# One split of 2,048 columns instead of two of 1,024 for each half chunk of expert weights

## The chip, the cores and the metric

The kernel runs on one core of one Trainium2 chip. A core has TensorE (PE in the profile; PEld is its weight load, which overlaps the matmuls), VectorE (DVE), ScalarE (ACT), GpSimd (POOL) and SyncE (SP, which issues the transfers), each with its own instruction stream; 16 DMA engines move data. The metric is the time of one execution in microseconds (us). Before the change it is 2620.03 us, the median of three runs between 2617.26 and 2626.58. One more execution was profiled; it took 2622.45 us, of which 2620.7 us is the span from the first to the last instruction and 1.75 us lies around it.

## The reference, cut to what matters

The program is a backbone of two layers over 256 context and 256 latent tokens of width 1024, in float32. Each layer mixes tokens and then channels; in the second layer the channel mixer is a set of eight experts, of which each token uses two. Only the experts matter here:

```python
D_MODEL, SEQ, N_EXPERTS, TOP_K, D_EXPERT = 1024, 256, 8, 2, 3584

def swiglu(h, w1, w3, w2):
    return (jax.nn.silu(h @ w1) * (h @ w3)) @ w2

def moe_swiglu(h, router, w1, w3, w2):
    logits = (h @ router).astype(jnp.float32)
    top_v, top_i = lax.top_k(logits, TOP_K)
    top_w = jax.nn.softmax(top_v, axis=-1)
    comb = jnp.einsum("blk,blke->ble", top_w,
                      jax.nn.one_hot(top_i, N_EXPERTS, dtype=jnp.float32)).astype(h.dtype)
    out = comb[..., 0:1] * swiglu(h, w1[0], w3[0], w2[0])
    for e in range(1, N_EXPERTS):
        out = out + comb[..., e:e + 1] * swiglu(h, w1[e], w3[e], w2[e])
    return out
```

Here h holds the 256 latent tokens. w1 and w3 are 1024 x 3584 for each expert and w2 is 3584 x 1024, so the eight experts have 352 MB of float32 weights, each read once.

## The kernel before, in words

The experts' stage is the last one of the program. It begins at about 1566 us of the span and ends with a short normalisation. The experts are taken in order of their number of tokens. Position 0, the largest, has up to 192 tokens in two groups, one of 128 and one of 64; positions 1 to 3 have up to 128, positions 4 to 7 up to 64. `gather` collects an expert's tokens with matmuls against a 0/1 matrix and casts them to two parts, a high and a low one. A group of 128 tokens is called heavy here; its high and low part are two tiles. A group of 64 is called light: both parts lie side by side in one tile of 128 columns.

Each expert is worked in seven chunks of 512 hidden columns. A chunk needs w1, w3 and w2 of these columns, two megabytes each, and each of them comes as two half chunks of 128 x 2048 float32 (one megabyte). That makes 6 loads for a chunk, 42 for an expert and 336 in all. `mload` is called once for each: SP issues the transfer into a landing tile `mland` (5 buffers), and `split` (lines 113 and 114) makes two tiles of the float32 data that a fast matmul can take: ScalarE casts it to the high part `mwh`, then VectorE subtracts this from the source and writes the rest, `mwl`. Before the change this is done in two steps of 1,024 columns, with 8 buffers for each of the two names. A buffer of `mwh` or `mwl` comes free when the last matmul that reads it is done, and only then can the cast of a later half begin.

TensorE multiplies the tokens by both parts. A heavy group takes three matmuls of 512 columns for each slice of weights (`mm3`, lines 121 to 123: high x high, high x low, low x high), a light group two (line 1152). One half of 1,024 columns carries 6 heavy or 4 light matmuls. `up1` multiplies by w1 and ScalarE copies the result out (line 1172 heavy, line 1174 light). `up3` multiplies by w3; for a light group ScalarE copies it out (line 1191), TensorE folds the two parts with 16 short matmuls (line 1195), ScalarE applies the silu (line 1198), VectorE multiplies (line 1199) and the product is split (`gh`). `down` multiplies by w2 into `y`. `back` spreads the sums back to the tokens.

The order of the work is not written out by hand. `steps` walks positions 1, 4, 2, 5, 3, 6, 7 so that `down` of a chunk stands behind `up1` of the next, and `experts` puts the fourteen steps of position 0 (`steps0`, whose `down` holds both half chunks of w2 for both groups) between those of the light positions. Then the tile framework's scheduler, which runs a cost model of its own, sets the order of the instructions in each engine's stream, and each engine works its stream strictly in that order.

Of the kernel before, what the change touches and what calls it, by code (L numbers as in the profile page):

```python
# [11 lines left out]
FR = mybir.dt.float32r  # L12
# [68 lines left out]
class Net:  # L81
# [1051 lines left out]
    def mload(self, src):  # L1133

        nc, p = self.nc, self.ep
        w = p.tile([128, 2048], FT, name="mland", tag="mland", bufs=5)
        nc.sync.dma_start(w, src)
        r = []
        for q in range(2):
            h = p.tile([128, 1024], FR, name="mwh", tag="mwh", bufs=8)  # L1140
            lo = p.tile([128, 1024], FR, name="mwl", tag="mwl", bufs=8)
            self.split(h, lo, w[:, q * 1024:(q + 1) * 1024])
            r.append((h, lo))
        return r

    def mmx(self, o, x, i, w, start, stop):

# [426 lines left out]
```

## Time and profile before

| what | value |
|---|---|
| median of 3 runs | 2620.03 us |
| profiled execution | 2622.45 us |
| its span | 2620.7 us |
| experts' stage | about 1566 to 2608 us of the span |
| PE busy, whole span | 2370.6 us, 90% |
| DVE busy, whole span | 2159.9 us, 82% |
| ACT busy, whole span | 1374.9 us, 52% |
| transfers of expert weights | 336 of 1 MB, median 6.5 us from issue to landing |

The busy share of an engine is an average over the whole program; what a change in the experts' stage can do is read from stretches inside it, and from what ended each idle time there. A matmul's row gives an end that is modelled, and neighbouring matmuls overlap, so the distance between two starts is what TensorE really spends on one. The same holds, to a smaller degree, for instructions of VectorE and ScalarE that stand back to back.

### The profile page before, as it was taken

The numbers are of one execution on the slowest core, as the hardware profiler recorded it, in microseconds if no ns is written. First come the engines' busy times: TensorE is split into PE (matmuls) and PEld (weight loads), VectorE is DVE, ScalarE is ACT, GpSimd is POOL, SyncE is SP. The second block draws the span as 40 slices with busy tenths as digits, with TensorE's granted clock in tenths as the row PEclk, the third lists the DMA queues.
The fourth block names the chain that finished last, engine by engine and source line by source line (L and its number), as shares of the span: only waits on it lengthen the run. The fifth ranks groups of instructions, "written<-read, shape, count | busy, mean of one in ns | idle before, by whom it ended". The sixth has DMA issues, their size and how long they took to land. (4 is left out here: it accounts for less than half of the span.)

```text
span 2620.7 us, 35146 instructions
## 1 busy us (share of the span) xinstructions
PE 2370.6 (90%) x12456; PEld 1947.5 (74%) x12456; DVE 2159.9 (82%) x3182; ACT 1374.9 (52%) x1965; POOL 190.1 (7%) x210
## 2 busy tenths in 40 slices
PE   7968978999999999987878969999999999999986
PEld 2746765788777877767768968888888788888775
DVE  8877699974767988976889678888988889898897
ACT  3334332323353233324544527777877677787864
POOL 1540000000100023221000010000000000000000
PEclk8978988999999999998989978999999999999988
DMA  6555423652234556674544529998899889999984
GB/s 239 165 181 113 145 89 125 205 161 82 96 91 159 179 163 193 204 244 115 175 137 130 178 86 348 356 358 335 344 353 350 326 332 344 354 361 365 359 325 203
DMA packets 157017, 594.11 MB, mean 227 GB/s; under 512 B 46423, under 2 KB 55321, under 8 KB 113825
## 3 DMA queue, kind: packets, MB, share of 16 engines
q1 hardware_dynamic: 156832, 591.79, 64.0%
q8 instruction: 99, 1.62, 0.2%
q14 instruction: 86, 0.70, 0.1%
HBM read 560.29 MB, written 31.42 MB: 226 GB/s over the span
## 5 line engine op out<-in xcount | busy, mean ns | idle before, releaser
L114 DVE TENSOR_TENSOR mwl<-mland,mwh 128x1024 fp32r<-128x1024 f32 x672 | 788.8, 1220 | 83.1 <-ACT mwh L113 71.6
L113 ACT CAST mwh<-mland 128x1024 fp32r<-128x1024 f32 x672 | 675.6, 1051 | 131.2 <-PE mp L123 42.0
L113 ACT CAST wh<-land 128x512 fp32r<-128x512 f32 x396 | 244.9, 621 | 525.7 <-PE p L122 238.2
L114 DVE TENSOR_TENSOR wl<-land,wh 128x512 fp32r<-128x512 f32 x396 | 294.5, 748 | 133.4 <-ACT wh L113 130.1
L121 PE MATMUL p<-hh,wh 128*128 128x256 f32 (+1 forms) x800 | 274.9, 345 | 7.4 <-DVE q L547 3.0
L123 PE MATMUL p<-hh,wl 128*128 128x256 f32 (+1 forms) x800 | 273.7, 344 | 2.8 <-DVE wl L114 2.7
L122 PE MATMUL p<-hl,wh 128*128 128x256 f32 (+1 forms) x800 | 272.6, 342 | 0.1
L1152 PE MATMUL mp<-mwl,xg 128*128 128x512 f32 x560 | 224.3, 403 | 4.2 <-DVE mwl L114 4.2
L1152 PE MATMUL mp<-mwh,xg 128*128 128x512 f32 x560 | 222.6, 400 | 3.3 <-ACT mwh L113 2.6
L121 PE MATMUL mp<-mwh,xg 128*128 128x512 f32 x448 | 179.4, 401 | 2.6 <-ACT mwh L113 2.6
L122 PE MATMUL mp<-mwl,xg 128*128 128x512 f32 x448 | 178.3, 398 | 2.2 <-DVE mwl L114 2.2
L123 PE MATMUL mp<-mwh,xg 128*128 128x512 f32 x448 | 176.7, 394 | 0.0
L121 PEld LDWEIGHTS p<-hh,wh 128*128 128x128 f32 x800 | 155.2, 194 | 27.8 <-ACT wh L113 3.9
L785 DVE SCALAR_TENSOR_TENSOR ma<-mw,sv,ma 128x512 f32<-128x512 f32 x196 | 150.5, 792 | 28.4 <-DMA mw<-in_w_mod 28.1
L123 PEld LDWEIGHTS p<-hh,wl 128*128 128x128 f32 x800 | 154.3, 193 | 22.9 <-DVE wl L114 5.5
L122 PEld LDWEIGHTS p<-hl,wh 128*128 128x128 f32 x800 | 154.8, 194 | 15.7 <-DVE hl L749 0.3
L123 PE MATMUL fo<-hh,wl 128*128 128x512 f32 (+1 forms) x384 | 146.9, 384 | 6.6 <-DVE wl L114 6.6
L121 PE MATMUL fo<-hh,wh 128*128 128x512 f32 (+1 forms) x384 | 146.9, 383 | 1.4 <-ACT hh L745 0.9
L122 PE MATMUL fo<-hl,wh 128*128 128x512 f32 (+1 forms) x384 | 145.6, 380 | 0.0
L667 DVE SCALAR_TENSOR_TENSOR dc<-ub,cfp,dc 128x512 f32<-128x512 f32 (+1 forms) x240 | 138.2, 614 | 0.5
L1152 PEld LDWEIGHTS mp<-mwl,xg 128*128 128x128 f32 x560 | 107.3, 192 | 27.4 <-DVE mwl L114 6.6
L1152 PEld LDWEIGHTS mp<-mwh,xg 128*128 128x128 f32 x560 | 107.3, 192 | 24.7 <-ACT mwh L113 4.5
(462 smaller groups left out, 4717.4 us busy)
## 6 DMA issues: line engine op xcount, KB each, us to landing
mland<-in_moe_w SPq DMA_DIRECT2D x336, 1024.0 KB, 6.5
mw<-in_w_mod SPq DMA_DIRECT2D x96, 512.0 KB, 4.5
land<-in_w_in SPq DMA_DIRECT2D x96, 512.0 KB, 4.3
land<-in_ffn_w SPq DMA_DIRECT2D x66, 512.0 KB, 3.6
land<-in_w_bo SPq DMA_DIRECT2D x24, 512.0 KB, 3.4
s5wc<-sw SPq DMA_DIRECT2D x16, 512.0 KB, 3.9
s5we<-weT SPq DMA_DIRECT2D x16, 512.0 KB, 3.6
we<-s5we SPq DMA_DIRECT2D x16, 512.0 KB, 4.4
```

The source lines that it names most:

```text
L113: nc.scalar.copy(h, src)
L114: nc.vector.tensor_sub(lo, src, h.bitcast(FT))
L121: nc.tensor.matmul(o, a[0], b[0], start=start, stop=False)
L122: nc.tensor.matmul(o, a[0], b[1], start=False, stop=False)
L123: nc.tensor.matmul(o, a[1], b[0], start=False, stop=stop)
L667: nc.vector.scalar_tensor_tensor(d, ub[:, :R, i:i + 64], cfp[:, j, i:i + 1], d, op0=OP.mult, op1=OP.add)
L785: nc.vector.scalar_tensor_tensor(ac[:, t], wk, self.sv[:, k, t:t + 1], ac[:, t], op0=OP.mult, op1=OP.add)
L1152: self.nc.tensor.matmul(o, x[0][:, i], w[r], start=start and r == 0, stop=stop and r == 1)
```

## The change: one cast and one subtraction over the whole half chunk

`mload` now makes one `mwh` and one `mwl` tile of 2,048 columns and splits the landing tile in one step. It hands its callers the two halves of these tiles as slices, so the matmuls read the same values as before. The number of buffers goes from 8 of 1,024 columns to 4 of 2,048 for each name, which is the same memory. There are 336 casts and 336 subtractions instead of 672 of each.

```diff
         w = p.tile([128, 2048], FT, name="mland", tag="mland", bufs=5)
         nc.sync.dma_start(w, src)
-        r = []
-        for q in range(2):
-            h = p.tile([128, 1024], FR, name="mwh", tag="mwh", bufs=8)
-            lo = p.tile([128, 1024], FR, name="mwl", tag="mwl", bufs=8)
-            self.split(h, lo, w[:, q * 1024:(q + 1) * 1024])
-            r.append((h, lo))
-        return r
+        h = p.tile([128, 2048], FR, name="mwh", tag="mwh", bufs=4)
+        lo = p.tile([128, 2048], FR, name="mwl", tag="mwl", bufs=4)
+        self.split(h, lo, w)
+        return [(h[:, q:q + 1024], lo[:, q:q + 1024]) for q in (0, 1024)]
```

The function is three lines shorter, so what stands below it has a line number smaller by three: the copies of lines 1174 and 1191 are lines 1171 and 1188 in the changed kernel, the silu of 1198 is 1195, the product of 1199 is 1196. The scheduler plans again with the new instructions, and from the start of the stage on the streams of TensorE, ScalarE and VectorE stand in another order; in SP's stream only one load of weights changes places with a small load near the end. Three places follow.

The first is VectorE's stream at the start of the stage, from the first subtraction of weights on; the short rows between are the tail of the routing. Before:

```order
L114 TENSOR_TENSOR mwl<-mland,mwh 128x1024
L1092 TENSOR_REDUCE rkp_13564<-cp 128x1
L114 TENSOR_TENSOR mwl<-mland,mwh 128x1024
L1091 TENSOR_TENSOR cp<-eq,cbp_13565 128x8
L1092 TENSOR_REDUCE cbp_13566<-cp 128x1
```

The same place in the changed kernel:

```order
L114 TENSOR_TENSOR mwl<-mland,mwh 128x2048
L1092 TENSOR_REDUCE cbp_13566<-cp 128x1
L1084 TENSOR_SCALAR eq<-iota,ix 128x8
L1085 TENSOR_TENSOR ov<-ov,eq 128x8
L1087 TENSOR_TENSOR cp<-eq,od 128x8
```

The first low part is now made by one instruction over both halves, and no short work stands between them.

The second is ScalarE's stream a little into the first light position, where steps of position 0 stand between. Before:

```order
L1172 ACTIVATE ms<-mp 128x512
L113 CAST mwh<-mland 128x1024 x2
L1174 COPY ms<-mp 128x512
L113 CAST mwh<-mland 128x1024 x2
L1174 COPY ms<-mp 128x512
L113 CAST mwh<-mland 128x1024 x6
L1191 COPY ms_15252<-mp 128x512
L113 CAST mwh<-mland 128x1024 x2
L1198 ACTIVATE ms_15252<-gtp 128x256
```

The same place in the changed kernel:

```order
L1169 ACTIVATE ms<-mp 128x512
L113 CAST mwh<-mland 128x2048 x2
L1171 COPY ms<-mp 128x512
L113 CAST mwh<-mland 128x2048 x2
L1171 COPY ms<-mp 128x512
L113 CAST mwh<-mland 128x2048 x4
L1188 COPY ms_15036<-mp 128x512
L113 CAST mwh<-mland 128x2048
L1195 ACTIVATE ms_15036<-gtp 128x256
```

Between the copies that wait for TensorE stand casts of 2, 2 and 4 loads where there were casts of 1, 1 and 3; the copies keep their order.

The third is the end of the stage, the last chunk of position 7, first on ScalarE. Before:

```order
L1174 COPY ms<-mp 128x512
L113 CAST mwh<-mland 128x1024 x6
L1191 COPY ms_22617<-mp 128x512
L113 CAST mwh<-mland 128x1024 x2
L1198 ACTIVATE ms_22617<-gtp 128x256
L113 CAST gh<-ms_22617 128x4x64
```

The same place in the changed kernel:

```order
L1171 COPY ms<-mp 128x512
L113 CAST gh<-ms_21177 128x4x64
L113 CAST mwh<-mland 128x2048 x2
L1188 COPY ms_21281<-mp 128x512
L1195 ACTIVATE ms_21281<-gtp 128x256
L113 CAST gh<-ms_21281 128x4x64
```

The cast of the last load stands ahead of the copy of line 1191 (now 1188) and no longer between it and the silu. On VectorE the rows there were:

```order
L1199 TENSOR_TENSOR ms_22489<-ms_22489,gtp 128x256
L114 TENSOR_TENSOR mwl<-mland,mwh 128x1024 x2
L114 TENSOR_TENSOR gh<-ms_22489,gh 128x4x64
L114 TENSOR_TENSOR mwl<-mland,mwh 128x1024 x8
L1199 TENSOR_TENSOR ms_22617<-ms_22617,gtp 128x256
```

and in the changed kernel they are:

```order
L1196 TENSOR_TENSOR ms_21177<-ms_21177,gtp 128x256
L114 TENSOR_TENSOR mwl<-mland,mwh 128x2048
L114 TENSOR_TENSOR gh<-ms_21177,gh 128x4x64
L114 TENSOR_TENSOR mwl<-mland,mwh 128x2048 x2
L1196 TENSOR_TENSOR ms_21281<-ms_21281,gtp 128x256
```

The last product stands behind the last subtraction in both; one load's split has moved to an earlier place.

## Rows read from the trace of the kernel before

**Rows 1.** Windows: busy us of each engine, granted clock, DMA share, GB/s.

```profile
core 0: us, PE busy (x) PEld busy (x) DVE busy (x) ACT busy (x) POOL busy (x), PEclk, DMA share, GB/s
1600.00:2400.00 800.00, 787.24 (x3753) 656.04 (x3751) 700.77 (x705) 610.11 (x713) 0.00 (x0) 0.99 0.92 345
2400.00:2592.00 192.00, 177.12 (x838) 144.66 (x838) 174.06 (x178) 148.91 (x184) 0.00 (x0) 0.95 0.90 348
2552.00:2559.00 7.00, 6.69 (x19) 5.30 (x19) 7.00 (x9) 3.60 (x5) 0.00 (x0) 0.56 1.02 411
```

**Rows 2.** Waits, 1600 to 2592 us: us in total, times, longest.

```profile
DVE mwl L114 <- ACT mwh L113: 66.8, 88, 3.2
ACT mwh L113 <- PE mp L123: 38.9, 96, 1.8
...
ACT mwh L113 <- PE y L1152: 32.2, 16, 7.1
```

**Rows 3.** Timeline of PE: start, us, instruction, idle before and its releaser.

```profile
1758.75 0.74 PE L1152 MATMUL y<-mwl,gh 128*128 128x512 f32 x2 [0.34 <-DVE mwl L114]
...
1863.63 0.39 PE L123 MATMUL mp<-mwh,xg 128*128 128x512 f32 x1
...
1865.67 0.39 PE L123 MATMUL mp<-mwh,xg 128*128 128x512 f32 x1
...
1917.16 0.51 PE L121 MATMUL mp<-mwh,xg 128*128 128x512 f32 x1 [1.18 <-ACT mwh L113]
...
1918.42 0.50 PE L122 MATMUL mp<-mwl,xg 128*128 128x512 f32 x1 [0.76 <-DVE mwl L114]
...
2552.31 0.80 PE L1152 MATMUL mp<-mwl,xg 128*128 128x512 f32 x1 [2.58 <-DVE mwl L114]
2552.91 0.63 PE L1152 MATMUL mp<-mwh,xg 128*128 128x512 f32 x1
...
2557.60 0.63 PE L1152 MATMUL mp<-mwh,xg 128*128 128x512 f32 x1
```

**Rows 4.** Groups by line and shape: busy us, mean ns of one, idle before.

```profile
L114 DVE TENSOR_TENSOR mwl<-mland,mwh 128x1024 fp32r<-128x1024 f32 x672 | 788.8, 1220 | 83.1 <-ACT mwh L113 71.6 <-PE mp L1152 3.6 <-PE y L123 1.2
L113 ACT CAST mwh<-mland 128x1024 fp32r<-128x1024 f32 x672 | 675.6, 1051 | 131.2 <-PE mp L123 42.0 <-PE y L1152 32.2 <-PE mp L1152 32.2
...
L114 DVE TENSOR_TENSOR gl<-gtp,gh 128x512 fp32r<-128x512 f32 x28 | 19.2, 685 | 5.0 <-ACT gh L113 4.9
...
L113 ACT CAST gh<-gtp 128x512 fp32r<-128x512 f32 x28 | 16.5, 588 | 5.2 <-PE gtp L1187 4.7
```

**Rows 5.** Timeline of ACT and DVE: casts and subtractions back to back.

```profile
1849.36 6.74 ACT L113 CAST mwh<-mland 128x1024 fp32r<-128x1024 f32 x7
...
1850.48 13.71 DVE L114 TENSOR_TENSOR mwl<-mland,mwh 128x1024 fp32r<-128x1024 f32 x12
```

**Rows 6.** Waits of SP's own queue, 1560 to 2600 us.

```profile
SPq L1137 <- DVE mwl L114: 674.0, 276, 12.1
```

**Rows 7.** Timeline at the first load of the stage.

```profile
1571.49 2.00 ACT L113 CAST mwh<-mland 128x1024 fp32r<-128x1024 f32 x2 [1.77 <-DMA mland<-in_moe_w]
...
1572.57 1.23 DVE L114 TENSOR_TENSOR mwl<-mland,mwh 128x1024 fp32r<-128x1024 f32 x1 [1.93 <-ACT mwh L113]
...
1574.89 0.63 PE L122 MATMUL mp<-mwl,xg 128*128 128x512 f32 x1
```

**Rows 8.** Timeline at the last chunk of the stage.

```profile
2589.75 0.59 ACT L1191 COPY ms<-mp 128x512 f32<-128x512 f32 x1 [2.91 <-PE mp L1152]
2590.23 1.99 ACT L113 CAST mwh<-mland 128x1024 fp32r<-128x1024 f32 x2
...
2591.31 2.36 DVE L114 TENSOR_TENSOR mwl<-mland,mwh 128x1024 fp32r<-128x1024 f32 x2 [2.28 <-ACT mwh L113]
2592.12 0.39 ACT L1198 ACTIVATE ms<-gtp 128x256 f32<-128x256 f32 x1
2593.59 0.41 DVE L1199 TENSOR_TENSOR ms<-ms,gtp 128x256 f32<-128x256 f32 x1
```

## The prediction

> **What bounds the kernel now.** The change touches the experts' stage alone, so I read that stage first, by windows. Between 1600 and 2400 us TensorE is busy for 787.24 of 800 us, VectorE for 700.77, ScalarE for 610.11, and the transfers run at 345 GB/s; between 2400 and 2592 us TensorE is busy for 177.12 of 192 us and VectorE for 174.06 [rows 1]. The first stretch is TensorE's: 12.8 us of it are idle. In the second TensorE has 14.9 us idle and VectorE has 17.9, so there the two share the bound. No engine can give more than TensorE's idle time, 27.7 us in both.
>
> Then the waits. ScalarE's casts wait for TensorE to free a buffer (the two largest groups are 38.9 and 32.2 us), and VectorE's subtractions wait for the casts, 66.8 us [rows 2]. That is the picture of a ring that is full most of the time: the split runs ahead of TensorE and is held back by it. A shorter split is worth nothing in such a moment.
>
> Last, TensorE's own timeline, for the moments in which the ring was empty. Between 1600 and 2592 us it waited for mwh or mwl 13 times, at 10 places, for 12.0 us in sum; the first and the last of these are the ones at 1758.75 and 2552.31 [rows 3]. At 1917.16 one sees the whole pattern: a wait of 1.18 us for the cast, one matmul, and a wait of 0.76 us for the subtraction behind that cast. These places are where the length of one cast and one subtraction stands on the path.
>
> **What becomes shorter.** 336 casts and 336 subtractions go. A subtraction of 512 columns takes 685 ns and one of 1,024 takes 1220 (the former reads PSUM), so 535 ns for 512 more columns; 2,048 columns should take 1220 + 2 x 535 = 2290 ns [rows 4]. Twelve back to back take 13.71 us, which is (13.71 - 1.22) / 11 = 1.135 us from start to start, 0.085 less than one alone [rows 5]. From start to start the new one costs 2.290 - 0.085 = 2.205 us against 2 x 1.135 = 2.270: 0.065 us less for a load. For the cast, 588 and 1051 ns give 1051 + 2 x 463 = 1977 ns [rows 4]; seven in 6.74 us are 0.948 us apart [rows 5], so 1.977 - 0.103 = 1.874 against 1.896, 0.02 us less. In the whole stage VectorE gains 336 x 0.065 = 22 us and ScalarE 7 us.
>
> The Trainium skill ("Perfetto Trace Analysis", section Optimizing Scalar/DVE Operations) puts the cost of one more instruction at about 60 ns for VectorE and 93 ns for ScalarE, both on SBUF, and says that larger operations improve throughput if the engine is saturated. For VectorE the trace agrees, 65 ns; for ScalarE rows of this kernel make it 20 ns; by the page's figures the sums would be 20 and 31 us.
>
> How much of the 22 us stands on the path? Before 2400 us I count nothing: TensorE's work hides it. After 2400 us VectorE shares the bound; 348 GB/s over 192 us [rows 1] are 66.8 MB or 64 loads: 64 x 0.065 = 4.2 us gained. The ends are 0 and 22 us; I take 4.2, since the row of the last stretch is the only one that shows VectorE near its limit.
>
> **What becomes longer.** From a landed load to its first high part it now takes one cast of 1.98 instead of 1.05 us, 0.93 more. To the first low part it takes 1.98 + 2.29 = 4.27 instead of 1.05 + 1.22 = 2.27 us, 2.0 more. To the last low part it took 2.27 + 1.135 = 3.4 us, so 0.9 more. Where TensorE already waits for a cast or a subtraction, it will wait for this. At 10 places that is between 10 x 0.93 = 9.3 and 10 x 2.0 = 20 us; it is 0 where the new plan puts other matmuls into the gap. I take 0.93 a place, 9.3 us, the row nearest to a sure loss: the second of the two waits is in part repaid, since the second half of the load then is ready at once.
>
> The ring also gets coarser. While TensorE works one load, only three others can stand ready or in work, where up to seven halves could; a buffer comes free at the end of a load and not in its middle. A light load is 8 matmuls. From 1863.63 to 1865.67 nine starts of matmuls lie 0.227 us apart [rows 3], so a light load is 1.8 us of TensorE and three are 5.4 us, which must cover 4.27 us for the new split and whatever stands before it on ScalarE and VectorE. Seven halves of 0.9 us were 6.3 us for 2.27. The slack falls from 4.0 to 1.1 us in a run of light matmuls. It is still positive, so I count no new places in the forecast, and leave them to the rival.
>
> At the start the first cast begins at 1571.49, the first subtraction at 1572.57, and TensorE takes the first low part at 1574.89 [rows 7]. With the new sizes that low part is ready at 1571.49 + 1.98 + 2.29 = 1575.8: 0.9 us late. Everything behind it moves by that, as TensorE is then busy without a gap.
>
> At the end the plan wins something. ScalarE waited 2.91 us in front of the copy at 2589.75, and the last two casts stood behind that copy; so the product of line 1199, whose input was there at 2592.12 + 0.39 = 2592.5, had to wait for two subtractions until 2593.59 [rows 8]. In the new order the cast of 1.98 us stands ahead of the copy and fits into that idle time; the product can begin at 2592.55: 1.0 us gained.
>
> The transfers: 276 waits of SP for a subtraction sum to 674 us, since a load is issued when VectorE has freed one of five landing tiles [rows 6]. A landing tile is freed by its last subtraction before and after, 0.9 us later for a lone load and no later in a backlog. As casts wait for TensorE's buffers rather than for data, I count nothing; if transfers became the bound, it would be up to 1 us at the same 10 places, inside the range. One load of weights is issued ahead of a small load near the end and not behind it, which changes nothing here.
>
> **The sum,** against the profiled execution of 2622.45 us: -4.2 + 9.3 + 0.9 - 1.0 = +5.0, so 2627.4. That execution lies 2.4 us above the median of the three runs (2620.03), so for a median I say 2625: 0.2% slower than 2620.03, which is within 0.3%, about 7.9 us and the least that a measurement of this kernel can tell from no change.
>
> **The rivals.**
> *The ring runs dry.* With the slack of a light run down to 1.1 us, a copy in ScalarE's stream that waits for TensorE, or a sum on VectorE, is enough to empty it, and TensorE waits at new places. The wait also has a second price. After the one of 2.58 us at 2552.31, the matmuls from 2552.91 to 2557.60 start 0.43 us apart and not 0.227 (11 steps in 4.69 us), and the stretch 2552 to 2559 has a granted clock of 0.56 [rows 1, 3], so most of it ran at the lower level of 1.2 GHz after TensorE had stood idle: 11 x 0.2 = 2.2 us more. One place at its worst costs 2.0 + 2.2 = 4.2 us. It decides, by the 7.9 us above, once the places sum to 12.2 us, which is three at this price. All ten at 4.2 us are 42, less the gains of 5.2 and with 0.9 for the start, +38: 2658. Half of it, +19, is 2639. For it: ten dry places exist already. Against it: the 13 waits of before are 0.9 us on average, and the matmul after the one of 1.18 us lasts 0.51 us by its row, not 0.63 as the slow ones do [rows 3]. Chance 0.35.
>
> The Trainium skill speaks for this rival in the same page and section: if ScalarE and VectorE are not saturated but cause bubbles on other engines, breaking up instructions may let work be completed sooner. The change does the reverse; the two waits at 1917.16 and 1918.42 are such a bubble.
>
> *VectorE is the limit in all light stretches,* not only after 2400 us, and TensorE's 27.7 us of idle time are its work. Then up to 22 us go: 2620 - 22 = 2598; with half of it, 2609. For it: VectorE is busy 88% of the long stretch, and it loses time waiting for casts that it can't make good. Against it: TensorE's waits for mwl and mwh are only 12.0 us, so no more than these can go by a faster split, and 12 with the tail's 1 less the start's 1 is 2608. Chance 0.22.
>
> *The change is a change of plan more than of sizes:* TensorE's stream differs nearly everywhere in the stage, and a new order of matmuls may be better or worse by several us whatever a cast costs. This has no sign of its own, and widens both sides by some 5 us; I give it no chance apart.
>
> **How the numbers follow.** Forecast (2613 to 2627) 0.43, dry ring 0.35, VectorE's limit 0.22. The last two are slower and faster by over 0.3%. The range leaves out a tenth on each side: down to 2608, which is all that the waits for the split can give, and up to 2646, between half and all of the dry ring. Faster 0.22, same 0.43, slower 0.35.
>
> **What would show it.** Subtractions of 2.28 to 2.30 and casts of 1.95 to 2.0 us; VectorE busy about 22 us less. TensorE's waits for mwl and mwh: 18 to 26 us in sum for the forecast, over 35 with more stretches at the lower clock for the dry ring, under 8 for VectorE's limit. The product of the last chunk should begin right after its silu. I am wrong if the stage gets longer with these waits unchanged (then the plan or the transfers did it), or if VectorE's idle time behind casts grows by more than its busy time falls.

## The result and the profile after

The changed kernel takes 2679.34 us (median of 4 runs, 2675.53 to 2681.97) against 2620.33 us of the kernel before (now the median of four): a ratio of 1.0222, 95% interval 1.0206 to 1.0238. It is 2.2% or 59 us slower; 2625 was forecast, with a range to 2646.

The page of the changed kernel has the instructions that were taken away, and their time. Its first part gives busy us of each engine and the number of instructions, its fifth the groups with busy us, the mean ns of one, and the idle time before them:

```profile
span 2673.7 us, 34167 instructions
...
PE 2380.7 (89%) x12456; PEld 1949.7 (73%) x12456; DVE 2134.9 (80%) x2846; ACT 1336.4 (50%) x1629; POOL 188.7 (7%) x210
...
L114 DVE TENSOR_TENSOR mwl<-mland,mwh 128x2048 fp32r<-128x2048 f32 x336 | 760.1, 2288 | 180.4 <-ACT mwh L113 176.9
L113 ACT CAST mwh<-mland 128x2048 fp32r<-128x2048 f32 x336 | 635.6, 1911 | 247.5 <-PE mp L1149 111.2
```

VectorE is busy 25 us less than before (2159.9), as the change meant it to be. But beside [rows 4] the last columns are what counts: the subtractions' idle time behind casts went from 71.6 to 176.9 us, nearly four times the 28.7 us by which their busy time fell (788.8 to 760.1), and the casts' idle time before them from 131.2 to 247.5. TensorE's busy time rose by 10.1 us and its idle time in the span by 42.9 (2673.7 - 2380.7 = 293.0, before 250.1); these two are the 53.0 us by which the span grew.

By stretches, with the columns of [rows 1]:

```profile
1600.00:2400.00 800.00, 757.62 (x3559) 623.84 (x3559) 650.96 (x420) 553.15 (x428) 0.00 (x0) 0.99 0.88 331
2400.00:2592.00 192.00, 172.06 (x807) 141.43 (x806) 152.75 (x108) 129.18 (x110) 0.00 (x0) 0.95 0.86 316
```

In the long stretch TensorE was idle 12.8 us and is now idle 42.4; VectorE had 700.77 us of work there and has 650.96, the transfers run at 331 and not 345 GB/s. All engines and the transfers do less at once: nobody is the bound more than before, they wait for each other.

Who waits for whom, on all engines between 1600 and 2640 us (us in total, times, longest), beside [rows 2]:

```profile
DVE mwl L114 <- ACT mwh L113: 171.3, 121, 6.1
ACT mwh L113 <- PE mp L1149: 109.8, 59, 6.9
ACT mwh L113 <- PE mp L123: 60.9, 50, 4.1
```

and on TensorE alone, between 1570 us and the end, first before the change:

```profile
PE mp L1152 <- DVE mwl L114: 4.2, 4, 2.6
...
PE mp L121 <- ACT mwh L113: 2.6, 2, 1.5
PE mp L1152 <- ACT mwh L113: 2.6, 3, 1.6
PE mp L122 <- DVE mwl L114: 2.2, 3, 0.9
...
PE y L121 <- ACT gh L113: 0.7, 1, 0.7
...
PE y L1152 <- DVE mwl L114: 0.3, 1, 0.3
```

and in the changed kernel:

```profile
PE mp L1149 <- DVE mwl L114: 26.9, 10, 6.1
PE mp L122 <- DVE mwl L114: 14.2, 10, 2.4
PE y L121 <- ACT gh L113: 10.3, 6, 2.5
PE mp L121 <- ACT mwh L113: 3.2, 3, 2.3
PE y L1149 <- ACT mwh L113: 3.1, 2, 1.6
...
PE y L1149 <- DVE mwl L114: 1.2, 1, 1.2
PE mp L1149 <- ACT mwh L113: 1.1, 1, 1.1
```

In the changed kernel the three rows for mwl have 42.3 us and the three for mwh 7.4: TensorE stood 27 times for 49.7 us where it stood 13 times for 12.0 us, and most of it for the low part, which is made last.

One such place shows how it comes about. The three fences are ScalarE, VectorE and TensorE of the changed kernel in one run of light work (start, us, instruction, times; in brackets the idle time before it and what ended it):

```profile
2422.47 3.73 ACT L113 CAST mwh<-mland 128x2048 fp32r<-128x2048 f32 x2 [3.17 <-PE y L1149]
2427.24 5.57 ACT L113 CAST mwh<-mland 128x2048 fp32r<-128x2048 f32 x3 [1.04 <-PE y L1149]
2432.71 0.58 ACT L1188 COPY ms<-mp 128x512 f32<-128x512 f32 x1
2433.18 3.71 ACT L113 CAST mwh<-mland 128x2048 fp32r<-128x2048 f32 x2
```

```profile
2424.42 4.49 DVE L114 TENSOR_TENSOR mwl<-mland,mwh 128x2048 fp32r<-128x2048 f32 x2 [2.89 <-ACT mwh L113]
2428.83 1.28 DVE L1299 TENSOR_TENSOR macc<-macc,y 128x512 f32<-128x512 f32 x2
2430.03 11.09 DVE L114 TENSOR_TENSOR mwl<-mland,mwh 128x2048 fp32r<-128x2048 f32 x5
```

```profile
2435.14 0.50 PE L1149 MATMUL mp<-mwh,xg 128*128 128x512 f32 x1
2438.97 0.79 PE L1149 MATMUL mp<-mwl,xg 128*128 128x512 f32 x1 [3.32 <-DVE mwl L114]
2439.56 0.63 PE L1149 MATMUL mp<-mwh,xg 128*128 128x512 f32 x1
```

The ring is full, so the cast stands idle for 3.17 us until TensorE frees a buffer at 2422.47, and VectorE stands idle behind it. Then the subtraction has to wait for the whole cast: it starts 1.95 us after it. From 2430.03 on VectorE subtracts without a gap and does not catch up: five take 11.09 us, 2.2 us a load, while a light load is 1.8 us of TensorE. At 2435.14 TensorE takes a high part whose low part comes 3.8 us later. VectorE can't keep pace in a light run by its own speed, and could not before (2.27 us a load, by the prediction); it lives on what it made in advance, and by this reading of one place the idle time in front of 2424.42 is what it lacks in the end. Behind the wait the matmul's row says 0.63 us and not 0.39. The stretch from 2438 to 2446 us has a granted clock of 0.57, most of it at the level of 1.2 GHz, after TensorE had stood idle:

```profile
2438.00:2446.00 8.00, 7.03 (x22) 5.64 (x22) 5.58 (x4) 2.86 (x3) 0.00 (x0) 0.57 1.00 383
```

The start of the stage went as worked out. In the changed kernel

```profile
1569.93 1.90 ACT L113 CAST mwh<-mland 128x2048 fp32r<-128x2048 f32 x1 [1.78 <-DMA mland<-in_moe_w]
...
1574.21 0.79 PE L122 MATMUL mp<-mwl,xg 128*128 128x512 f32 x1 [0.69 <-DVE mwl L114]
```

TensorE takes the first low part 4.28 us after the first cast began, and before 3.40 us after it [rows 7]: 0.9 us more.

### The profile page after: what moved, and what is told of

The parts are those of the page before. It is cut to its first block, busy times and chain, and to the rows that moved or that the text cites. A ratio compares the mean times of both kernels' runs of the same rounds, so it can differ in the third digit from the quotient of the medians.

```text
span 2673.7 us, 34167 instructions
## 1 busy us (share of the span) xinstructions
PE 2380.7 (89%) x12456; PEld 1949.7 (73%) x12456; DVE 2134.9 (80%) x2846; ACT 1336.4 (50%) x1629; POOL 188.7 (7%) x210
## 5 line engine op out<-in xcount | busy, mean ns | idle before, releaser
L114 DVE TENSOR_TENSOR mwl<-mland,mwh 128x2048 fp32r<-128x2048 f32 x336 | 760.1, 2288 | 180.4 <-ACT mwh L113 176.9
L113 ACT CAST mwh<-mland 128x2048 fp32r<-128x2048 f32 x336 | 635.6, 1911 | 247.5 <-PE mp L1149 111.2
L1149 PE MATMUL mp<-mwl,xg 128*128 128x512 f32 x560 | 229.3, 411 | 27.3 <-DVE mwl L114 26.9
L122 PE MATMUL mp<-mwl,xg 128*128 128x512 f32 x448 | 178.9, 399 | 14.2 <-DVE mwl L114 14.2
```

The source lines that it names most:

```text
L113: nc.scalar.copy(h, src)
L114: nc.vector.tensor_sub(lo, src, h.bitcast(FT))
L122: nc.tensor.matmul(o, a[0], b[1], start=False, stop=False)
L1149: self.nc.tensor.matmul(o, x[0][:, i], w[r], start=start and r == 0, stop=stop and r == 1)
```

## The experiments

Three theories were at hand. R: the ring is coarser, since a buffer of 2,048 columns comes free only at the end of a load. T (first called L): it takes longer until the first low part of a load is there. P: the scheduler's new order is worse. In all kernels the matmuls and their values are the same.

**Coarse tiles, short instructions.** Two splits of 1,024 columns as before, in tiles of 2,048 with 4 buffers. The framework keeps track of the halves, so a matmul on the first half waits for the first cast alone: in the trace both of TensorE's waits for `mwh` end 0.05 us after the first cast of a load.

```diff
-        h = p.tile([128, 2048], FR, name="mwh", tag="mwh", bufs=4)
-        lo = p.tile([128, 2048], FR, name="mwl", tag="mwl", bufs=4)
-        self.split(h, lo, w)
-        return [(h[:, q:q + 1024], lo[:, q:q + 1024]) for q in (0, 1024)]
+        H = p.tile([128, 2048], FR, name="mwh", tag="mwh", bufs=4)
+        L = p.tile([128, 2048], FR, name="mwl", tag="mwl", bufs=4)
+        r = [(H[:, q:q + 1024], L[:, q:q + 1024]) for q in (0, 1024)]
+        for q in range(2):
+            self.split(*r[q], w[:, q * 1024:(q + 1) * 1024])
+        return r
```

> Two casts and two subtractions of 1,024 columns as before the change, but written into tiles of 2,048 columns with 4 buffers as after it; a matmul on the first half waits only for the first cast. Theory R (the ring: a buffer comes free only at the end of a load, and 4 buffers hold less than 8): most of the loss stays, ratio to before 1.013 to 1.022, TensorE's waits for mwh and mwl 30 us or more. Theory L (the length: the first low part is ready 2 us later): 0.998 to 1.005, waits near 12 us. Theory P (only the new order of the streams): any ratio, with no relation to the waits.

Measured: 2623.75 us, ratio 1.0006 (0.9988 to 1.0023). The whole loss is gone, with buffers that come free as in the changed kernel: no second cast of a load waits for TensorE any more (0 of 336), where in the kernel before 82 did. R falls in the form in which it was put. The order of the streams is also new here, and costs nothing. TensorE's waits for the two parts are 16.8 us:

```profile
PE mp L1151 <- DVE mwl L114: 10.4, 10, 3.6
...
PE mp L122 <- DVE mwl L114: 2.6, 4, 1.5
PE mp L1151 <- ACT mwh L113: 2.0, 1, 2.0
PE mp L121 <- ACT mwh L113: 1.5, 1, 1.5
PE y L1151 <- DVE mwl L114: 0.3, 1, 0.3
```

**Only the cast wide.**

```diff
-        h = p.tile([128, 2048], FR, name="mwh", tag="mwh", bufs=4)
-        lo = p.tile([128, 2048], FR, name="mwl", tag="mwl", bufs=4)
-        self.split(h, lo, w)
-        return [(h[:, q:q + 1024], lo[:, q:q + 1024]) for q in (0, 1024)]
+        H = p.tile([128, 2048], FR, name="mwh", tag="mwh", bufs=4)
+        self.nc.scalar.copy(H, w)
+        r = []
+        for q in (0, 1024):
+            lo = p.tile([128, 1024], FR, name="mwl", tag="mwl", bufs=8)
+            h = H[:, q:q + 1024]
+            self.nc.vector.tensor_sub(lo, w[:, q:q + 1024], h.bitcast(FT))
+            r.append((h, lo))
+        return r
```

> One cast of 2,048 columns into a tile with 4 buffers, then two subtractions of 1,024 columns into 8 separate low tiles. First low part after 1.91 + 1.22 = 3.1 us (before 2.3, after 4.2). L: about 0.4 of the loss, ratio 1.007 to 1.011. R: the high tiles are as coarse as in the changed kernel and gate the cast, so 1.013 to 1.022.

Measured: 2633.54 us, ratio 1.0048 (1.0034 to 1.0062), less than T expected and far from R. The cast of 2,048 columns costs some 13 us by itself.

**Only the subtraction wide.** Tiles and slices as in the first kernel.

```diff
-        for q in range(2):
-            self.split(*r[q], w[:, q * 1024:(q + 1) * 1024])
+        for q in range(2):
+            self.nc.scalar.copy(r[q][0], w[:, q * 1024:(q + 1) * 1024])
+        self.nc.vector.tensor_sub(L, w, H.bitcast(FT))
```

> Two casts of 1,024 columns, then one subtraction of 2,048, both into tiles of 2,048 with 4 buffers. High part after 1.05 us as before the change, first low part after 2.0 + 2.29 = 4.3 us as after it. L: like the changed kernel, 1.018 to 1.024, since nearly all its waits are for mwl. R: 1.013 to 1.022, the same as the kernel with two of each in coarse tiles, from which it should not differ by more than 0.004.

Measured: 2685.34 us, ratio 1.0231 (1.0197 to 1.0266): the whole loss, from the subtraction that waits for both casts. R had expected no difference from the coarse tiles with short instructions; there are 2.2%.

**Short subtractions in the wrong order.** To tell a long instruction on VectorE from a late low part, both subtractions have 1,024 columns, but the second half's comes first. H in the expectation is the theory that short work on VectorE stands behind the long instruction.

```diff
-        self.nc.vector.tensor_sub(L, w, H.bitcast(FT))
+        sub = lambda q: nc.vector.tensor_sub(r[q][1], w[:, q * 1024:(q + 1) * 1024], r[q][0].bitcast(FT)).ins
+        s = sub(1)
+        with self.tc.issue_after(s):
+            sub(0)
```

> Tiles of 2,048 columns with 4 buffers, two casts and two subtractions of 1,024 columns, but the subtraction of the second half is issued first, so the first low part is ready after 2.0 + 1.13 + 1.22 = 4.3 us, as in the changed kernel, while no instruction of VectorE is longer than 1.22 us. Theory T (time to the first low part decides): 1.016 to 1.024 and TensorE's waits for mwh and mwl over 40 us. Theory H (short work on VectorE stands behind an instruction of 2.29 us): like the kernel with short instructions in coarse tiles, 0.998 to 1.006, waits under 20 us.

Measured: 2700.45 us, ratio 1.0311 (1.0280 to 1.0341), more than T expected. So the loss does not need a long instruction on VectorE, as H has it; a late first low part is enough. TensorE's waits on the part are

```profile
PE mp L1155 <- DVE mwl L1143: 32.3, 17, 4.7
PE mp L122 <- DVE mwl L1143: 17.4, 12, 3.4
```

Why it is some 21 us worse than the changed kernel (2700.45 and 2679.34 us), with the first low part at about the same time, was not settled. VectorE is busy 782.6 us with these subtractions and not 760.1, which would be of that size, but no run sets this apart.

**A shallower ring.** The kernel before, 6 buffers for 8.

```diff
-            h = p.tile([128, 1024], FR, name="mwh", tag="mwh", bufs=8)
-            lo = p.tile([128, 1024], FR, name="mwl", tag="mwl", bufs=8)
+            h = p.tile([128, 1024], FR, name="mwh", tag="mwh", bufs=6)
+            lo = p.tile([128, 1024], FR, name="mwl", tag="mwl", bufs=6)
```

> The kernel before with 6 buffers of 1,024 columns for mwh and mwl and not 8: three loads in place of four, split and freed by halves. R: the depth counts, so slower by 1.01 or more, with ScalarE's waits for TensorE well above the 119 us of before. L: 1.000 to 1.006.

Measured: 2664.92 us, ratio 1.0169 (1.0138 to 1.0199). T alone did not expect this (1.000 to 1.006), R did (1.01 or more): with the split as short as before, one load less of cover costs 44 us. Depth and split time are two sides of one account.

**A deeper ring for the changed kernel.** Five buffers of 2,048 columns, with the room taken from other rings, and the kernel before with the same smaller rings as its control.

```diff
-        w = p.tile([128, 2048], FT, name="mland", tag="mland", bufs=5)
+        w = p.tile([128, 2048], FT, name="mland", tag="mland", bufs=4)
...
-        h = p.tile([128, 2048], FR, name="mwh", tag="mwh", bufs=4)
-        lo = p.tile([128, 2048], FR, name="mwl", tag="mwl", bufs=4)
+        h = p.tile([128, 2048], FR, name="mwh", tag="mwh", bufs=5)
+        lo = p.tile([128, 2048], FR, name="mwl", tag="mwl", bufs=5)
```

(and `xg` 7 for 8, `g` 2 for 3; the control has these two and mland 4, with the splits of the kernel before)

> The changed kernel with 5 buffers of 2,048 columns for mwh and mwl and not 4; the room is taken from mland (4 for 5), xg (7 for 8) and g (2 for 3). Five buffers give one more light load of cover, 1.8 us or more, which is about what the long split takes more. If time to the first low part matters only against the cover that the ring gives: at least half of the loss comes back against the next kernel, 1.000 to 1.011 of it. If not: 1.018 to 1.024 of it. A shortage of landing tiles would show as DMA waits of the casts.

> The kernel before with the same smaller rings (mland 4, xg 7, g 2), its own 8 buffers of 1,024 columns: what these alone cost. All theories: 1.000 to 1.012, from the landing tiles above all.

Measured: 2642.22 us, ratio 1.0075 (1.0045 to 1.0105), and for the control 2634.56 us, 1.0062 (1.0042 to 1.0083). Against its control the wide split now costs 7.7 us by the medians (1.0029), which the two intervals do not tell from nothing, and not 59. VectorE's idle time behind casts falls from 176.9 to 131.6 us (70.0 in the control), and the casts wait for transfers instead (108.5 us, 41.8 in the control with the same four landing tiles):

```profile
L114 DVE TENSOR_TENSOR mwl<-mland,mwh 128x2048 fp32r<-128x2048 f32 x336 | 763.2, 2289 | 138.4 <-ACT mwh L113 131.6
L113 ACT CAST mwh<-mland 128x2048 fp32r<-128x2048 f32 x336 | 638.8, 1912 | 210.9 <-DMA mland<-in_moe_w 108.5
```

**Smaller pieces.** Four splits of 512 columns in coarse tiles, run twice, and one kernel with pieces of 512, 512 and 1,024.

```diff
-        for q in range(2):
-            self.split(*r[q], w[:, q * 1024:(q + 1) * 1024])
+        for q in range(4):
+            c = slice(q * 512, (q + 1) * 512)
+            self.split(H[:, c], L[:, c], w[:, c])
```

```diff
+        for c in (slice(0, 512), slice(512, 1024), slice(1024, 2048)):
+            self.split(H[:, c], L[:, c], w[:, c])
```

> Four casts and four subtractions of 512 columns for each load, in tiles of 2,048 columns with 4 buffers. The first low part is ready after 0.59 + 0.69 = 1.3 us (before 2.3); VectorE pays 4 x 0.60 = 2.40 us for a load and not 2.27, 44 us in the stage. T: the waits of 12 us can fall by half, but the last stretch pays some 64 x 0.13 = 8 us: 0.996 to 1.004. If VectorE's busy time decided: 1.008 to 1.02.

> The kernel with four splits of 512 columns again, with more rounds, to tell whether it beats the kernel before: its first comparison gave 0.9983 with an interval of 0.9967 to 1.0. Expected 0.997 to 1.000.

> Three splits for each load, of 512, 512 and 1,024 columns, in tiles of 2,048 with 4 buffers. First low part after 1.3 us as with four splits of 512, VectorE 2 x 0.60 + 1.13 = 2.33 us for a load (2.27 before, 2.40 with four). T, with VectorE's time as the only price: a little under the kernel before and under four splits, 0.995 to 0.999. If the two cancel: 0.998 to 1.002.

Measured for four: 2617.68 us, ratio 0.9983 (0.9967 to 1.0000), and again 2620.59 us, 0.9991 (0.9980 to 1.0001). For three: 2621.85 us, 1.0002 (0.9990 to 1.0013). None can be told from the kernel before; for three T had expected 0.995 to 0.999. Four cost VectorE 40 us more of busy time for the subtractions (828.9 us for 788.8) and take nothing from the total: its time is not the bound, nor does a still earlier low part gain: TensorE's waits for the two parts are 14.0 us, where T had let them fall to half of 12.

The kernels with room for four loads in one table (time to the first low part from the mean durations of the casts and subtractions, with two in a row counted by their distance; loss from the ratio, times 2620 us):

| split | first low part | VectorE busy with it | loss |
|---|---|---|---|
| four of 512 | 1.3 us | 829 us | -2 and -4 us, not clear |
| two of 1,024, coarse tiles | 2.3 us | 784 us | 2 us, not clear |
| wide cast, two subtractions | 3.1 us | 782 us | 13 us |
| changed kernel | 4.2 us | 760 us | 58 us |
| two casts, wide subtraction | 4.3 us | 761 us | 61 us |
| two of each, second half first | 4.3 us | 783 us | 81 us |

The loss follows the first column and not the second, and it is not a line: the cover of the ring takes up the first steps, and then hardly anything. VectorE's idle time behind casts goes nearly the same way, from top to bottom 52, 86, 122, 177, 171 and 180 us.

P was not tested by itself: the scheduler made a plan for every kernel, and a part of the loss may be the plan's. Two things in the traces speak against a large part. TensorE's order in the stage is about equally far from the changed kernel's in the kernel with the wide cast and in the one with the second half first (some 370 of 4,760 matmuls out of order in each), and these lose 13 and 81 us. And the changed plan has no longer runs of light work on weights: the longest are 248 and 200 matmuls, before 263 and 193.

## Why the prediction was wrong

**The sizes of the instructions were right.** 2288 ns for a subtraction (2290 worked out), 1911 for a cast (1977, and 1.95 to 2.0 us said; so a little shorter), VectorE busy 25 us less (22). From start to start five subtractions in 11.09 us are 2.20 us apart, 0.07 less for a load than 2 x 1.135, as worked out; on the path this was worth nothing. The Trainium skill ("Perfetto Trace Analysis", section Optimizing Scalar/DVE Operations) has about 60 ns for one more instruction on VectorE on SBUF; the distances agree with it. For ScalarE the 20 ns were too few: two casts in 3.73 us are 1.82 us apart and not 1.896, 76 ns less.

**The step that failed** is in "What becomes longer": "The slack falls from 4.0 to 1.1 us in a run of light matmuls. It is still positive, so I count no new places in the forecast". The cover was counted as three whole loads and the price as one split on idle engines. But VectorE needs 2.2 us for a load and a light load is 1.8 us of TensorE, so in a light run the cover shrinks with each load; what counts is how far ahead VectorE is when the run begins, and the idle time behind a whole cast takes that away. (That the lead is what is lost is argued from the one place above and borne out by the deeper ring; it was not followed load by load.) The waits went from 13 at 10 places to 27 at 25. A wait was 0.9 us on average and is 1.84 (49.7 / 27). That this is again 0.93 us more is luck: the 0.93 was meant for each of the ten old places, and most of the waits are new. So the term for waits, taken as +9.3 us, measured +37.8 us; TensorE's busy time, which no term of the forecast had (the dry ring's second price comes near it), gives 10.1 us more, and the two together are 47.9 of the 53 us of span. Most of the rest, 4.3 us, lies in TensorE's other waits, 25.6 us in sum and 21.3 before; the largest of them is for the high part of `gh`, 10.3 us for 0.7.

**The gain of 4.2 us after 2400 us** did not come. VectorE was busy 21 us less there, mostly because 57 loads fell into it and not 64, and TensorE's idle time went from 14.9 to 19.9 us: VectorE was near its limit by its busy share, but what TensorE lacked was an early low part.

**The start** cost 0.9 us, as worked out.

**The end** did not gain in the way worked out. The product of the last chunk starts right behind its silu, as predicted, but the last cast, now ahead of the copy, waits itself 1.43 us for a buffer, and the copy stands behind it:

```profile
2641.81 1.91 ACT L113 CAST mwh<-mland 128x2048 fp32r<-128x2048 f32 x1 [1.43 <-PE mp L1149]
2643.63 0.57 ACT L1188 COPY ms<-mp 128x512 f32<-128x512 f32 x1
...
2646.56 0.38 ACT L1195 ACTIVATE ms<-gtp 128x256 f32<-128x256 f32 x1 [2.36 <-PE gtp L1192]
```

and on VectorE:

```profile
2646.97 0.42 DVE L1196 TENSOR_TENSOR ms<-ms,gtp 128x256 f32<-128x256 f32 x1 [0.93 <-ACT ms L1195]
```

The idle time in front of the copy, which the cast was to use, went into the wait for a buffer. TensorE meanwhile does sixteen matmuls of `y` from 2641.84 us on, and its wait for the last `gh` is 1.89 us and was 3.46; whether the end as a whole gained by that was not settled.

**The rival** with the dry ring was the right one in its signs: waits over 35 us, and more stretches at the lower clock. From 1560 us on there are 13 such stretches with work of TensorE in them and were 9, and TensorE is busy in them for 50.6 us and was for 41.4. The forecast's own sign of being wrong came too: "VectorE's idle time behind casts grows by more than its busy time falls". The rival's mechanism was half right. The coarser freeing of buffers, which it named first, costs nothing alone (1.0006). The late low part against the ring's cover does, and a deeper ring pays most of it back. Even its 2658 us was too low, as it multiplied the old ten places. The rival in which VectorE is the limit falls by the four splits of 512 columns, which give it 40 us more work at no cost.

The Trainium skill ("Perfetto Trace Analysis", section Optimizing Scalar/DVE Operations) has both rules in one place: larger operations improve throughput if the engine is saturated, and breaking up instructions may let work finish sooner if an engine is not saturated but causes bubbles on others. Here the second one governs, as the coarse tiles with short instructions (1.0006) against the changed kernel (1.0222) show; VectorE at 88% in the long stretch was not saturated enough for the first.

## What to carry to other kernels

Two engines that work on one tile in turn overlap only across its pieces: with one piece the second engine starts when the first has finished, and that time comes off the lead which the ring holds for the consumer. Before making instructions larger, compare the producer's time for a unit with the consumer's in the fastest stretch, not on average: where the producer is slower there, the lead is used up load by load, and a slack that is positive for one load says little. A price per old stall is a bound only if the number of stalls stays; here it doubled.

## What the runs showed of the hardware that was not expected

A short stall of TensorE can be paid twice: the stretch of 8 us after the wait of 3.32 us has a granted clock of 0.57. The clock fell with shorter waits too: after this one of 1.83 us most of the next 4 us ran at 1.2 GHz, while after the one of 2.39 us at 1787.70 the clock did not fall.

```profile
1888.49 0.62 PE L122 MATMUL mp<-mwl,xg 128*128 128x512 f32 x1 [1.83 <-DVE mwl L114]
```

```profile
1888.00:1892.00 4.00, 3.51 (x9) 2.73 (x10) 3.06 (x3) 0.81 (x1) 0.00 (x0) 0.59 1.02 430
```

In the whole span TensorE was busy 10.1 us longer with the same 12,456 matmuls. The lower clock is about 4 us of it, by an estimate: 9.2 us more of work at it (50.6 for 41.4), of which a share of 1 - 0.227 / 0.43 is due to the clock, by the distances of matmuls in the prediction. What the rest comes from stays open. VectorE's busy time with the subtractions fell by 28.7 us over 336 loads, 85 ns each, between the 65 ns worked out from start to start and the 152 ns of the mean durations (2 x 1220 - 2288).
